# On-chip values for the recurrence, raw x's buffer reused, and decay stored by heads, in a one-core transformer layer

## The chip, the core and the metric

The kernel runs on one core of a Trainium2 chip. A core has five engines with in-order queues: TensorE (PE, matmul; its weight loads are shown as PEld), VectorE (DVE), ScalarE (ACT), GpSimd (POOL) and SyncE (SP), whose queue here issues every DMA. An instruction waits at the head of its queue until the semaphores that it needs are set, and what stands behind it waits too. The metric is the device time of one execution in microseconds (us), the median of several runs.

## The reference

One layer of a hybrid trunk for a sequence of S = 1024 frames of width 1024, in float32. The parts that matter here:

```python
proj = x @ w_in        # q_a k_a v_a f_a | q_b f_b i_b g_b | gate_a gate_b
# attention, 8 heads of 64:
F = cumsum(log_sigmoid(f_a + b_f))                # per head, over frames
p = softmax(causal(q_t.k_s / 8 + F[t] - F[s]))    # y_a = p @ v_a
# recurrence, 4 heads of 128, v = i_b:
f = lb + (1 - lb) * sigmoid(f_b);  k = 1 - f
S_t = diag(f_t) S_{t-1} + k_t v_t^T;  o_t = S_t^T silu(q_t)
y_b = rms_norm(o) * norm_g * sigmoid(g_b)
merged = sigmoid(gate_a) * (y_a @ w_pa) + sigmoid(gate_b) * (y_b @ w_pb)
x = layer_norm(ALPHA * x + merged @ w_o)
x = layer_norm(ALPHA * x + (silu(g) * u) @ w_ff_out)   # u, g = x @ w_ff_in
```

The decay F of attention has one row of 1024 values for each of the 8 heads. Its row for a head is added to every score, so it must stand on all 128 partitions.

## The kernel before

Every matrix is split into a high and a low part (`split`: ACT casts the high part, DVE subtracts it to get the low part), and one product is three matmuls of 128x512 (`mm3`). Large products go by a two by two scheme with seven products (p1 to p7), whose operands are sums and differences of blocks of x and of the weights; DVE makes these. The names of operands: `xh`, `xl` are the parts of x's blocks, `vs1` to `vs4` those of sums of blocks, `T...h`, `T...l` those of weights. `vx`, `vy`, `qk_s`, `qk_pt` and so on are PSUM banks.

The stages, by the trace: projections of the two values (v_a into `va`, i_b into `vbm`) and the forget gates, 0 to 94 us; the q and k projection of head pair 0 (`qk_first`), to about 121; attention, 8 heads, to about 350; the recurrence, 4 heads (`hgrn_project`, `hgrn`), to about 585; gates, branch projections and output projection, to 841; the FFN, to the end. Gate projections (`gate`, PSUM banks `gps`) are also used as filler for TensorE between the products of attention and recurrence.

**What sets the order.** Nothing is issued as written. Each call is recorded by a planner (class `Plan`) with its data dependences, the buffers that it uses and an estimated duration. `schedule` then places the calls one at a time, always the one that can start first by its estimates; ties go by program order. `LAT` is the estimated time until another engine sees a result, `OWN` the same within an engine. Buffers come from slots with a count for each tag ("x" 5, "m" 1, "kb" 4 and so on), and a buffer is placed when a slot of its tag is free. The result is a fixed order for each engine's queue. All recorded calls are issued from one line, L279, so the profile's rows are told apart by the names of tiles.

What the change touches:

- `x2_r` (tag "x", 16 KB on each partition; rows `x_r` in the profile): raw x of the second half of the frames, blocks a21 and a22. The operands for p5, p6, p7 and p3 are made in it, and the splits of a21 for `qk_first` (`xl<-x_r,xh`) are its last use. `box1` (tag "m", four rows of 1024 values) holds the decay rows of attention in two halves, one for even and one for odd heads, and later the values and level buffers of the recurrence. The tag "m" has one slot, and `vbm` has it first.
- `forget_gates`: the forget gates are computed in 8 rows of 512, go through DRAM (`f_d`) to get to 64 rows of 128 (one for each block of 128 frames and head), and are summed along each row by a scan (`nf`). What the blocks ahead add is another sum over the last column: the column goes to DRAM (`b_d`, 64 values), comes back as rows (8 loads of 8x8), is multiplied by a constant table `before` and summed by DVE to `base`. Two more operations on 64x128 (`tensor_scalar` and `scalar_tensor_tensor`) give the decay, which is stored to `nf_d`. All these tiles read `f` in the profile.
- `attention`: for each head one DMA puts that head's decay on all 128 partitions (`box<-nf_d`), from `nf_d` in the order block, head, frame. POOL adds the causal mask to it (`box<-box,causal`), and DVE adds plain or masked decay to the scores: `p<-s,box`, a custom operation that also takes the row's maximum.
- the values of the recurrence: `vbm` is stored to `vb_d`, 8 stores of 256 KB, and each head of the recurrence loads its part into `box1` (512 KB).

Of the kernel before, what the change touches and what calls it, by code (L numbers as in the profile page):

```python
# [7 lines left out]
F32 = mybir.dt.float32  # L8
# [4 lines left out]
ALU = mybir.AluOpType  # L13
# [3 lines left out]
P = 128  # L17
# [35 lines left out]
class Plan:  # L53

    LAT = {"PE": 197.0, "ACT": 131.0, "DVE": 128.0, "POOL": 66.0, "SP": 1950.0}
    OWN = {"PE": 0.0, "ACT": 0.0, "DVE": 127.0, "POOL": 60.0, "SP": 1950.0}
    SETS = {AF.Exp: 0, AF.Ln: 0, AF.Sigmoid: 1, AF.Silu: 2}
# [223 lines left out]
def trunk(ctx: ExitStack, tc, a: dict, out: bass.AP):  # L283
# [175 lines left out]
    load(b22)  # L459
    ax = take("x", [2, 4, NB], "x2_r")  # L460
    a21, a22 = ([ax[:, i, c, :] for c in range(4)] for i in range(2))
    for c in range(4):
# [26 lines left out]

    nf_d = dram.tile([NT, HA, P], F32, name="nf_d")  # L490

    def forget_gates():
# [8 lines left out]
        split(wf[:, :, :HA], wf[:, :, LO:], wfx)  # L501
        f_d = dram.tile([NT, HA, P], F32, name="f_d")
        for hf, ops in enumerate(((A11, A12), (vops["p5"], A22))):
            fo = vx[1 + hf][:LO + HA]
            for c in range(KC):
                h, l = (x[c % 4] for x in ops[c // 4])
                w = wf[:, c + 4 * (hf and c > 3)]
                mm(fo, w, h, start=c == 0, stop=c == KC - 1)
                mm(fo[:HA], w[:, :HA], l, start=False, stop=c == KC - 1, skip_group_check=True)
            fs = half("gt", f"fs{hf}")[:HA]  # L510
            act.copy(fs, fo[LO:])
            dve.tensor_add(fs, fo[:HA], fs)
            sync.dma_start(f_d[4 * hf:4 * hf + 4].rearrange("t h p -> h t p"), fs.rearrange("h (t p) -> h t p", p=P))

# [3 lines left out]
        fz, fa, fe, fu = (f4[:, blk(i)] for i in range(4))  # L518
        sync.dma_start(fa, f_d.rearrange("t h p -> (t h) p"))
        act.activation(fe, fa, AF.Abs, bias=bf, scale=1.0)  # L520
# [34 lines left out]
    forget_gates()  # L555
    product("p5", T1, vy, True)
# [61 lines left out]
    def qk_project(p):  # L618
# [7 lines left out]
        return tiles  # L626

    box1 = take("m", [4, S], "box1")

# [43 lines left out]
    def attention(p, qk):  # L673
        q2, k2, kl = qk
        for i in range(2):
            h = 2 * p + i
            me = slice(i * DH, (i + 1) * DH)

            nfx = box1[:, 2 * (h % 2):2 * (h % 2) + 2, :].rearrange("p a (b c t) -> p (a b) c t", c=2, t=P)
            sync.dma_start(nfx[:, :, 1, :], nf_d[:, h, :].partition_broadcast(P))  # L680
            for hf in range(2):
                b4 = slice(4 * hf, 4 * hf + 4)
                pool.tensor_add(nfx[:, b4, 0, :].rearrange("p (j c) t -> p j c t", c=2),
                                nfx[:, b4, 1, :].rearrange("p (j c) t -> p j c t", c=2),
                                causal[:, None].to_broadcast([P, 2, 2, P]))
            vhl = take("hl", [NT, 2, DH], f"vhl{h}", F32R)
# [3 lines left out]
            for qb in range(NT):  # L690
# [5 lines left out]
                for ci, (c0, w) in enumerate(CHUNKS[qb]):  # L696
# [4 lines left out]
                    for o, m in ((0, w - tail), (w - tail, tail)):  # L701
                        if not m:
                            continue
                        b0, b1 = (c0 + o) // P, (c0 + o + m) // P
                        if o < w - tail:
                            add = nfx[:, b0:b1, 1, :]
                        elif m == P:
                            add = nfx[:, qb:qb + 1, 0, :]
                        else:
                            add = nfx.rearrange("p j c t -> p (j c) t")[:, 2 * qb - 1:2 * qb + 1, :]  # L710
# [804 lines left out]
def _constants():  # L1515
# [12 lines left out]
    t = np.arange(NT * HA)[:, None] // HA  # L1528
    b = np.arange(NT)
    before = np.zeros((NT * HA, NT + 2), np.float32)  # L1530
    before[:, :-2] = (b < t) | (b == t) & (t % 2 == 1)
    before[:, -2:] = np.concatenate([1 - 2 * (t % 2), t % 2], axis=1)
    return {"before": before, "ident": ident, "causal": causal, "once": once,
# [9 lines left out]
def _layout(x, w_in, b_fgate, hgrn_lb_logits, hgrn_norm_g, w_branch_a, w_branch_b, w_out, ln1_g, ln1_b,  # L1543
# [17 lines left out]
    def quarters(m):  # L1561
# [44 lines left out]
```

## Time and profile before

| | us |
|---|---|
| median of 3 runs | 1489.09 |
| lowest, highest run | 1487.78, 1489.48 |
| the profiled execution | 1488.35 |
| its span | 1486.6 |
| TensorE busy | 1455.0 |
| VectorE busy | 1107.8 |
| ScalarE busy | 677.6 |
| GpSimd busy | 99.1 |

The mean granted clock of TensorE over the execution is 0.994 of full speed. The profile is of one execution; its times count from the start of the span. A row of the timeline shows start, duration, engine, operation, the tiles (out<-in) and in brackets the idle time ahead of it with what ended it. A row "x3" stands for three like instructions in a row.

### The profile page before, as it was taken

The numbers are of one execution on the slowest core, as the hardware profiler recorded it, in microseconds if no ns is written. First come the engines' busy times: TensorE is split into PE (matmuls) and PEld (weight loads), VectorE is DVE, ScalarE is ACT, GpSimd is POOL, SyncE is SP. The second block draws the span as 40 slices with busy tenths as digits, with TensorE's granted clock in tenths as the row PEclk, the third lists the DMA queues.
The fourth block names the chain that finished last, engine by engine and source line by source line (L and its number), as shares of the span: only waits on it lengthen the run. The fifth ranks groups of instructions, "written<-read, shape, count | busy, mean of one in ns | idle before, by whom it ended". The sixth has DMA issues, their size and how long they took to land.

```text
span 1486.6 us, 19086 instructions
## 1 busy us (share of the span) xinstructions
PE 1455.0 (98%) x6805; PEld 1191.1 (80%) x6805; DVE 1107.8 (75%) x2090; ACT 677.6 (46%) x1163; POOL 99.1 (7%) x116
## 2 busy tenths in 40 slices
PE   9998999999999999999999899999999999999998
PEld 6766878888887887788888778888888888888887
DVE  7796686776887889744838898666666676798597
ACT  6536576677576575334511343333323323434330
POOL 0003231320001000000001000000000000000000
PEclk9999999999999999999999999999999999999999
DMA  7132232221112234446710203322333334976741
GB/s 261 31 115 79 64 69 48 60 80 40 43 52 77 66 131 157 151 141 212 265 61 1 113 19 117 103 100 102 107 106 106 106 107 170 345 266 219 253 162 58
DMA packets 83472, 177.04 MB, mean 119 GB/s; under 512 B 8816, under 2 KB 22064, under 8 KB 83376
## 3 DMA queue, kind: packets, MB, share of 16 engines
q1 hardware_dynamic: 83376, 175.81, 35.8%
q8 instruction: 54, 0.88, 0.2%
q14 instruction: 42, 0.34, 0.1%
HBM read 136.65 MB, written 39.13 MB: 118 GB/s over the span
## 4 chain that ended last, share of the span: by engine, by line
PE 84%; DVE 9%; DMA 4%; issue 1%; ACT 1%; SPq 1%; POOL 1%; DVEq 0%; ACTq 0%; POOLq 0%
PE p L279 14%; PE fb L279 11%; PE fa L279 8%; PE fc L279 8%; PE bps L279 8%; PE pps L279 6%; PE o L279 6%; PE gs L279 5%; PE gps L279 4%; PE pv L279 2%; PE kps L279 2%; PE s L279 2%; PE pt L279 2%; PE qps L279 2%; DMA b<-in_w_v 1%; PE lp L279 1%
## 5 line engine op out<-in xcount | busy, mean ns | idle before, releaser
L279 PE MATMUL p<-dp 128*128 128x512 f32 (+1 forms) x957 | 210.0, 382 | 0.0
L279 PEld LDWEIGHTS p<-dp 128*128 128x128 f32 x957 | 175.3, 188 | 34.8
L279 PE MATMUL fc<-xs,Tp 128*128 128x512 f32 x528 | 127.0, 389 | 0.0
L279 PE MATMUL fb<-xs,Tp 128*128 128x512 f32 x528 | 126.7, 389 | 0.0
L279 PE MATMUL fa<-x,Tp 128*128 128x512 f32 x480 | 115.7, 389 | 0.3 <-DVE u L279 0.3
L279 PEld LDWEIGHTS fc<-xs,Tp 128*128 128x128 f32 x528 | 99.1, 188 | 20.7 <-ACT xs L279 0.2
L279 PEld LDWEIGHTS fb<-xs,Tp 128*128 128x128 f32 x528 | 99.1, 188 | 20.6
L279 ACT CAST Tp<-t 128x512 fp32r<-128x512 f32 x88 | 54.5, 621 | 115.9 <-PE fc L279 72.6
L279 DVE TENSOR_TENSOR Tp<-t,Tp 128x512 fp32r<-128x512 f32 x88 | 60.7, 691 | 61.7 <-ACT Tp L279 61.2
L279 PEld LDWEIGHTS fa<-x,Tp 128*128 128x128 f32 x480 | 90.0, 188 | 19.3 <-ACT p L279 0.7
L279 ACT CAST dp<-dap 128x1024 fp32r<-128x1024 f32 (+1 forms) x42 | 41.2, 984 | 102.6 <-PE p L279 51.7
L279 PE MATMUL bps<-xl,wb_h 128*128 128x512 f32 x192 | 76.0, 396 | 0.0
L279 PE MATMUL bps<-xh,wb_h 128*128 128x512 f32 x192 | 75.9, 395 | 0.0
L279 PE MATMUL bps<-xh,wb_l 128*128 128x512 f32 x192 | 75.7, 396 | 0.0
L279 POOL TENSOR_TENSOR norm<-norm,mhalf 128x1 f32<-128x1 f32 x16 | 14.6, 914 | 883.8 <-DVE norm L279 883.8
L279 DVE TENSOR_TENSOR tl<-pt,th 128x512 fp32r<-128x512 f32 (+1 forms) x96 | 50.3, 552 | 16.6 <-ACT th L279 16.2
L279 DVE TENSOR_TENSOR dp<-dap,dp 128x1024 fp32r<-128x1024 f32 (+1 forms) x42 | 47.4, 1132 | 15.5 <-ACT dp L279 15.0
L279 POOL TENSOR_SCALAR p<-p,soft 128x384 f32<-128x384 f32 (+4 forms) x64 | 49.1, 772 | 130.2 <-DVE soft L279 113.4
L279 PE MATMUL fb<-x,Tp 128*128 128x512 f32 x240 | 57.7, 389 | 0.0
L279 ACT ACTIVATE p<-p,soft 128x384 f32<-128x384 f32 (+4 forms) x64 | 49.6, 777 | 13.2 <-DVE soft L279 12.9
L279 ACT CAST th<-pt 128x512 fp32r<-128x512 f32 (+1 forms) x96 | 42.9, 479 | 23.2 <-PE pt L279 21.9
L279 ACT CAST Tp<-wg_r 128x512 fp32r<-128x512 f32 x40 | 25.0, 624 | 62.0 <-PE fb L279 32.1
(511 smaller groups left out, 3528.0 us busy)
## 6 DMA issues: line engine op xcount, KB each, us to landing
dbp<-in_w_fo SPq DMA_DIRECT2D x45, 512.0 KB
dap<-a_d SPq DMA_DIRECT2D x35, 512.0 KB
a_d<-ar SPq DMA_DIRECT2D x42, 256.0 KB
wu_r<-in_w_ff SPq DMA_DIRECT2D x20, 512.0 KB
wg_r<-in_w_ff SPq DMA_DIRECT2D x20, 512.0 KB
a_d<-as SPq DMA_DIRECT2D x33, 256.0 KB
wg_r<-in_w_g SPq DMA_DIRECT2D x16, 512.0 KB
sg<-gate_d SPq DMA_DIRECT2D x32, 256.0 KB
```

The source lines that it names most:

```text
L279: getattr(q.engine, method)(*args, **kw)
```

## The change

- `box1` is now raw x's buffer from the start (tag "x", four rows of 1024: rows 0 and 1 hold a21, rows 2 and 3 a22). Even heads of attention use rows 2 and 3 for their decay (plain and masked), odd heads rows 0 and 1. In the recurrence all four rows are level buffers `e`, used in turn.
- `vbm` is read where it is; `vb_d`, its 8 stores and the 4 loads are gone. `vbm` keeps the only slot "m" until the last head's products.
- `f_d` and `nf_d` are stored as 8 rows of 1024. A broadcast reads one row of 4 KB for each partition, where it read 8 pieces of 512 B. The rows of `before`, `bf` and `nf` are sorted by head, then block.
- The round trip by `b_d`, the multiplication and the sum are replaced by one float32 matmul of the table `before` (64x64) with the last column. It goes into a bank of p1 to p7 (`vx[1]`), and is placed, with the two operations that use it, in the loop that ends p3.
- The planner's estimate for the latency of a DMA goes from 1950 to 2500 ns.

```diff
-    LAT = {... "SP": 1950.0}          # OWN the same
+    LAT = {... "SP": 2500.0}
...
-    ax = take("x", [2, 4, NB], "x2_r")
-    a21, a22 = ([ax[:, i, c, :] for c in range(4)] for i in range(2))
+    box1 = take("x", [4, S], "box1")
+    a21, a22 = ([box1[:, 2 * i + c // 2, hs(c % 2)] for c in range(4)] for i in range(2))
...
-    nf_d = dram.tile([NT, HA, P], F32, name="nf_d")
+    nf_d = dram.tile([HA, S], F32, name="nf_d")
...
-        b_d = dram.tile([NT, HA], F32, name="b_d")
-        sync.dma_start(b_d.rearrange("t h -> (t h)").unsqueeze(1), nf[:, P - 1:P])
         dve.tensor_sub(fz, fz, fa)
-        bs = fa[:, :NT]
-        for t in range(NT):
-            sync.dma_start(bs[t * HA:(t + 1) * HA], b_d.rearrange("t h -> h t"))
-        dve.tensor_mul(bs, bs, before[:, :NT])
-        base = fu[:, :1]
-        dve.tensor_reduce(base, bs, axis=mybir.AxisListType.X, op=ALU.add)
-        dve.tensor_scalar(fz, fz, before[:, NT + 1:NT + 2], base, op0=ALU.mult, op1=ALU.add)
-        dve.scalar_tensor_tensor(nf, nf, before[:, NT:NT + 1], fz, op0=ALU.mult, op1=ALU.add)
-        sync.dma_start(nf_d.rearrange("t h p -> (t h) p"), nf)
+        return nf, fz
+
+    def forget_sums(nf, fz):
+        BH = NT * HA
+        base = vx[1][:BH, :1]
+        mm(base, before[:, :BH], nf[:, P - 1:P], start=True, stop=True)
+        dve.tensor_scalar(fz, fz, before[:, BH + 1:BH + 2], base, op0=ALU.mult, op1=ALU.add)
+        dve.scalar_tensor_tensor(nf, nf, before[:, BH:BH + 1], fz, op0=ALU.mult, op1=ALU.add)
+        sync.dma_start(nf_d.rearrange("h (t p) -> (h t) p", p=P), nf)
...
         dve.tensor_add(p1v[t], vx[t], p1v[t])
+        if t == 1:
+            forget_sums(*forget)
         dve.tensor_add(va[:, 4 + t, :], va[:, 4 + t, :], p1v[t])
         dve.tensor_add(vbm[:, 4 + t, :], vbm[:, 4 + t, :], p1v[t])
-    vb_d = dram.tile([NT, P, NB], F32, name="vb_d")
-    for t in range(4, NT):
-        sync.dma_start(vb_d[t], vbm[:, t, :])
     for t in range(4):
         dve.tensor_add(vbm[:, t, :], vy[t], vbm[:, t, :])
-        sync.dma_start(vb_d[t], vbm[:, t, :])
...
-            sync.dma_start(nfx[:, :, 1, :], nf_d[:, h, :].partition_broadcast(P))
+            r = 2 - 2 * (h % 2)
+            nfx = box1[:, r:r + 2, :].rearrange("p a (b t) -> p (a b) t", t=P)
+            sync.dma_start(box1[:, r, :], nf_d[h].partition_broadcast(P))
...
-        vt = box1[:, h % 2, :]
-        sync.dma_start(vt.rearrange("p (t d) -> p t d", d=P), vb_d[:, :, h * P:(h + 1) * P].rearrange("t p d -> p t d"))
...
         def V(w):
-            return vt[:, blk(w)]
+            return vbm[:, w, blk(h)]
...
-            e = box1[:, 2 + li % 2, :]
+            e = box1[:, li % 4, :]
```

The planner turns this into other orders. Three places of the queues, before and after. The first is ACT's queue in `qk_first`, between the casts for q and for k of head pair 0 (`wq` and `wg` are weights of head pair 1 and of the first gate). Before:

```order
90 L279 ACTIVATE q_0_1_201<-qk_s 64x512
91 L279 CAST wq_h_365<-wq_r 128x512
92 L279 CAST k_0_0_202<-qk_u_195 64x512 x2
93 L279 CAST k_0_1_203<-qk_u_195 64x512
94 L279 CAST kl_0_204<-kl_0_204 64x512
```

Now:

```order
91 L279 ACTIVATE q_0_1_198<-qk_s 64x512
92 L279 CAST k_0_0_199<-qk_u_192 64x512 x2
93 L279 CAST k_0_1_200<-qk_u_192 64x512
94 L279 CAST kl_0_201<-kl_0_201 64x512
95 L279 CAST k_0_1_200<-qk_u_192 64x512
...
106 L279 ACTIVATE p_2_224,soft<-p_2_224,soft 128x384
107 L279 CAST wg_0_h_1119<-wg_0_r 128x512
108 L279 CAST wg_0_h_1121<-wg_0_r 128x512
109 L279 CAST wq_h_362<-wq_r 128x512
110 L279 CAST wq_h_364<-wq_r 128x512
111 L279 ACTIVATE p_3_227,soft<-p_3_227,soft 128x512
```

The cast of wq stood ahead of the k casts; both of its halves now stand 17 rows later, behind the casts for the first gate. The second place is DVE's queue around the sums of the forget gates (`f` is every tile of the gates). Before, among the sums for p7 and p3:

```order
93 L279 TENSOR_TENSOR x_r<-x_r,xl_69 128x512
94 L279 TENSOR_TENSOR x_r<-xh_67,x_r 128x512
95 L279 TENSOR_TENSOR f_128<-f_128,before 64x8
96 L279 TENSOR_TENSOR x_r<-xh_67,x_r 128x512
97 L279 TENSOR_REDUCE f_128<-f_128 64x1
98 L279 TENSOR_TENSOR vbm<-vx_73,p1v_106 128x512
99 L279 TENSOR_SCALAR f_128<-f_128,before 64x128
100 L279 TENSOR_TENSOR vs4l_167<-x_r,vs4h_165 128x512
101 L279 SCALAR_TENSOR_TENSOR f_128<-f_128,before 64x128
```

Now, behind the last add of p3 and ahead of the splits of a21:

```order
128 L279 TENSOR_TENSOR vbm<-vy_77,vbm 128x512
129 L279 TENSOR_TENSOR Tqkp2l<-wq_r,Tqkp2h 128x512
130 L279 TENSOR_TENSOR vbm<-vy_78,vbm 128x512
131 L279 TENSOR_SCALAR f_128<-f_128,before,vx_72 64x128
132 L279 SCALAR_TENSOR_TENSOR f_128<-f_128,before 64x128
133 L279 TENSOR_TENSOR xl_68<-box_104,xh_66 128x512 x3
```

The two operations that need the sums stand 32 rows later than before, and the product and the sum on DVE are gone. The third place is SP's queue from the loads for p3 on. Before:

```order
37 L279 DMA x_r<-in_xT 128x512 x2
38 L279 DMA b_d<-f_128 64x1
39 L279 DMA f_128<-b_d 8x8x1 x8
40 L279 DMA nf_d<-f_128 64x128
41 L279 DMA wq_r<-in_w_qk 128x1024
42 L279 DMA wk_r<-in_w_qk 128x1024
43 L279 DMA vb_d<-vbm 128x512 x8
44 L279 DMA box_181<-nf_d 128x8x128 x2
45 L279 DMA wq_r<-in_w_qk 128x1024
46 L279 DMA wg_0_r<-in_w_g 128x1024
```

Now:

```order
37 L279 DMA box_104<-in_xT 128x512 x2
38 L279 DMA wq_r<-in_w_qk 128x1024
39 L279 DMA wk_r<-in_w_qk 128x1024
40 L279 DMA nf_d<-f_128 64x128
41 L279 DMA box_104<-nf_d 128x1024 x2
42 L279 DMA wq_r<-in_w_qk 128x1024
43 L279 DMA wg_0_r<-in_w_g 128x1024
```

The round trip and the stores of `vbm` are gone, and the decay's store now stands behind the loads of the weights of head pair 0, right ahead of the broadcasts.

More of the change, by code (lines that the diff above doesn't have):

```diff
@@ L53 @@
 class Plan:
-    LAT = {"PE": 197.0, "ACT": 131.0, "DVE": 128.0, "POOL": 66.0, "SP": 1950.0}
-    OWN = {"PE": 0.0, "ACT": 0.0, "DVE": 127.0, "POOL": 60.0, "SP": 1950.0}
+    LAT = {"PE": 197.0, "ACT": 131.0, "DVE": 128.0, "POOL": 66.0, "SP": 2500.0}
+    OWN = {"PE": 0.0, "ACT": 0.0, "DVE": 127.0, "POOL": 60.0, "SP": 2500.0}
     SETS = {AF.Exp: 0, AF.Ln: 0, AF.Sigmoid: 1, AF.Silu: 2}
@@ L501, in forget_gates @@
         split(wf[:, :, :HA], wf[:, :, LO:], wfx)
-        f_d = dram.tile([NT, HA, P], F32, name="f_d")
+        f_d = dram.tile([HA, S], F32, name="f_d")
         for hf, ops in enumerate(((A11, A12), (vops["p5"], A22))):
@@ L512, in forget_gates @@
             dve.tensor_add(fs, fo[:HA], fs)
-            sync.dma_start(f_d[4 * hf:4 * hf + 4].rearrange("t h p -> h t p"), fs.rearrange("h (t p) -> h t p", p=P))
+            sync.dma_start(f_d[:, hs(hf)], fs)
         BH = NT * HA
@@ L518, in forget_gates @@
         fz, fa, fe, fu = (f4[:, blk(i)] for i in range(4))
-        sync.dma_start(fa, f_d.rearrange("t h p -> (t h) p"))
+        sync.dma_start(fa, f_d.rearrange("h (t p) -> (h t) p", p=P))
         act.activation(fe, fa, AF.Abs, bias=bf, scale=1.0)
@@ L531, in forget_gates @@
         dve.tensor_tensor_scan(nf, fz, fa, 0.0, op0=ALU.add, op1=ALU.subtract)
-        b_d = dram.tile([NT, HA], F32, name="b_d")
-        sync.dma_start(b_d.rearrange("t h -> (t h)").unsqueeze(1), nf[:, P - 1:P])
         dve.tensor_sub(fz, fz, fa)
-        bs = fa[:, :NT]
-        for t in range(NT):
-            sync.dma_start(bs[t * HA:(t + 1) * HA], b_d.rearrange("t h -> h t"))
-        dve.tensor_mul(bs, bs, before[:, :NT])
-        base = fu[:, :1]
-        dve.tensor_reduce(base, bs, axis=mybir.AxisListType.X, op=ALU.add)
-        dve.tensor_scalar(fz, fz, before[:, NT + 1:NT + 2], base, op0=ALU.mult, op1=ALU.add)
-        dve.scalar_tensor_tensor(nf, nf, before[:, NT:NT + 1], fz, op0=ALU.mult, op1=ALU.add)
-        sync.dma_start(nf_d.rearrange("t h p -> (t h) p"), nf)
+        return nf, fz
[6 more added lines that the diff above has]
+        sync.dma_start(nf_d.rearrange("h (t p) -> (h t) p", p=P), nf)
     bf = const("bf", [NT * HA, 1])
-    before = const("before", [NT * HA, NT + 2])
+    before = const("before", [NT * HA, NT * HA + 2])
     vops["p5"] = A21
@@ L554, in trunk @@
         split(vops["p5"][0][c], vops["p5"][1][c], s1)
-    forget_gates()
+    forget = forget_gates()
     product("p5", T1, vy, True)
@@ L626, in qk_project @@
         return tiles
-    box1 = take("m", [4, S], "box1")
     def qk_first():
@@ L677, in attention @@
             me = slice(i * DH, (i + 1) * DH)
-            nfx = box1[:, 2 * (h % 2):2 * (h % 2) + 2, :].rearrange("p a (b c t) -> p (a b) c t", c=2, t=P)
-            sync.dma_start(nfx[:, :, 1, :], nf_d[:, h, :].partition_broadcast(P))
+            r = 2 - 2 * (h % 2)
+            nfx = box1[:, r:r + 2, :].rearrange("p a (b t) -> p (a b) t", t=P)
+            sync.dma_start(box1[:, r, :], nf_d[h].partition_broadcast(P))
             for hf in range(2):
[L682 to L685, printed above, removed]
+                plain, masked = (nfx[:, b0 + 4 * hf:b0 + 4 * hf + 4].rearrange("p (j c) t -> p j c t", c=2) for b0 in (0, NT))
+                pool.tensor_add(masked, plain, causal[:, None].to_broadcast([P, 2, 2, P]))
             vhl = take("hl", [NT, 2, DH], f"vhl{h}", F32R)
@@ L705, in attention @@
                         if o < w - tail:
-                            add = nfx[:, b0:b1, 1, :]
+                            add = nfx[:, b0:b1]
                         elif m == P:
-                            add = nfx[:, qb:qb + 1, 0, :]
+                            add = nfx[:, NT + qb:NT + qb + 1]
                         else:
-                            add = nfx.rearrange("p j c t -> p (j c) t")[:, 2 * qb - 1:2 * qb + 1, :]
+                            add = nfx[:, qb - 1:NT + qb + 1:NT + 1]
                         res, got = (t.rearrange("p (a t) -> p a t", t=P) for t in (pt[:, c0 + o:c0 + o + m], sc[:, o:o + m]))
@@ L780, in hgrn_project @@
                     dve.tensor_mul(d, o, d)
-        return q, fk, sg, vt
+        return q, fk, sg
     def hgrn(h, qfg, box):
-        q, fk, sg, vt = qfg
+        q, fk, sg = qfg
         k = full("kb", f"hk{h}")
@@ L1527, in _constants @@
             lmask[:, c, nw - 1:2 * nw - 1] = (s[:, None] // (2 * L) == np.arange(nw)) & (s[:, None] // L % 2 == c)
[L1528 to L1532, printed above, removed]
+    bh = np.arange(NT * HA)
+    h, t = bh // NT, bh % NT
+    before = np.zeros((NT * HA, NT * HA + 2), np.float32)
+    before[:, :-2] = (h[:, None] == h) & ((t[:, None] < t) | (t[:, None] == t) & (t % 2 == 1))
+    before[:, -2], before[:, -1] = 1 - 2 * (t % 2), t % 2
     return {"before": before, "ident": ident, "causal": causal, "once": once,
@@ L1582, in _layout @@
         "w_fo": quarters(np.asarray(w_ff_out)[0]),
-        "bf": c(np.tile(np.asarray(b_fgate)[0], NT).reshape(NT * HA, 1)),
+        "bf": c(np.repeat(np.asarray(b_fgate)[0], NT).reshape(NT * HA, 1)),
         "lbl": c(np.asarray(hgrn_lb_logits)[0].reshape(HB, P).T),
```

## The prediction

> **What bounds the kernel now.** First the page: busy times, then the chain of work that ended last.
>
> ```profile
> PE 1455.0 (98%) x6805; PEld 1191.1 (80%) x6805; DVE 1107.8 (75%) x2090; ACT 677.6 (46%) x1163; POOL 99.1 (7%) x116
> PE 84%; DVE 9%; DMA 4%; issue 1%; ACT 1%; SPq 1%; POOL 1%; DVEq 0%; ACTq 0%; POOLq 0%
> ```
>
> TensorE (PE) is busy for 1455.0 of the span's 1486.6 us. No part of the change takes away large matmul work, so at most about 31 us of idle time, and matmuls that ran at a low clock, are there to be had. The second view is the stretches of the program: it shows where that time lies.
>
> ```profile
> 50.00:100.00 50.00, 47.19 (x204) 37.72 (x203) 40.05 (x80) 19.35 (x36) 0.00 (x0) 1.00 0.24 76
> 113.00:119.00 6.00, 0.47 (x3) 0.17 (x1) 1.35 (x2) 1.95 (x4) 2.26 (x2) 0.85 0.40 136
> 119.00:124.00 5.00, 4.83 (x13) 3.75 (x14) 3.70 (x11) 4.85 (x9) 0.00 (x0) 0.50 0.00 0
> 124.00:130.00 6.00, 4.52 (x21) 3.00 (x20) 4.79 (x17) 5.45 (x13) 1.85 (x3) 1.00 0.00 0
> 130.00:350.00 220.00, 219.03 (x1156) 177.62 (x1155) 158.61 (x545) 147.90 (x316) 61.38 (x73) 1.00 0.25 64
> 550.00:600.00 50.00, 48.37 (x254) 39.51 (x253) 48.77 (x95) 26.00 (x59) 3.23 (x2) 1.00 0.47 159
> 900.00:1270.00 370.00, 370.00 (x1634) 306.46 (x1633) 255.78 (x384) 120.33 (x197) 0.00 (x0) 1.00 0.34 113
> ```
>
> Columns: window, length, then busy us of PE, weight load, VectorE (DVE), ScalarE (ACT) and GpSimd (POOL), then granted clock, DMA share, GB/s. Read the first number after the comma. From 130 to 350 us (attention with gate matmuls as filler) and from 900 to 1270 us TensorE is never really idle: time won before 130 us is carried to the end, and work that DVE or DMA lose there is worth nothing. From 113 to 119 us it does almost nothing, and from 119 to 124 us it is busy at half the clock. The third view, PE's waits, names them:
>
> ```profile
> PE s L279 <- ACT k L279: 5.5, 1, 5.5
> PE fa L279 <- ACT Tp_0h L279: 4.1, 1, 4.1
> PE vx L279 <- DVE vbm L279: 1.9, 1, 1.9
> PE qk_s L279 <- DVE vbm L279: 0.8, 1, 0.8
> PE qk_pt L279 <- DVE qk_u L279: 0.7, 1, 0.7
> ```
>
> All but the second lie between 75 and 119 us. The change touches both their roots.
>
> **Term 1: the round trip of the block sums (b_d).** On DVE and SP (rows of the timeline):
>
> ```profile
> 61.49 0.41 DVE L279 TENSOR_TENSOR_SCAN f<-f 64x128 f32<-64x128 f32 x1
> 66.21 0.68 DVE L279 TENSOR_TENSOR x_r<-xh,x_r 128x512 f32<-128x512 f32 x1
> 68.28 2.73 SPq L279 DMA_DIRECT2D f<-b_d  x8
> 75.75 0.16 DVE L279 TENSOR_TENSOR f<-f,before 64x8 f32<-64x8 f32 x1 [8.86 <-DMA f<-b_d]
> 77.11 0.33 DVE L279 TENSOR_SCALAR f<-f,before 64x128 f32<-64x128 f32 x1
> 77.96 0.34 DVE L279 SCALAR_TENSOR_TENSOR f<-f,before 64x128 f32<-64x128 f32 x1
> 109.48 0.69 DVE L279 TENSOR_TENSOR qk_u<-qk_pt,qk_p 128x512 f32<-128x512 f32 x1
> 110.28 0.69 DVE L279 TENSOR_TENSOR qk_u<-qk_s,qk_u 128x512 f32<-128x512 f32 x1
> ```
>
> DVE's in-order queue stands 8.86 us before `f<-f,before`. Behind it are the `vbm<-vx` adds that free PE's banks (1.9 us of PE idle), then everything up to `qk_u`, which DVE works off late (0.8 and 0.7 us more). Changed, a 64x1 matmul gives the sums, and its two users stand some thirty rows later, behind the last `vbm<-vy`. DVE does not wait at 66.9 us any more. It then has about 8 us in hand, more than PE's three waits together, so these go: 1.9 + 0.8 + 0.7 = 3.4 us. From there PE sets the pace, and the second `qk_u` add, done at 110.97 us, is done at about 107.6. What the wait turns into: DVE now waits for the last `vy` product of p3 instead, which it must do in any order.
>
> The added matmul has no row in the trace. From below it costs nothing much (one column); from above, the x128 products `s<-k,q` below took 0.37 us each at half clock, and its inputs (the scan, done near 62 us, and the bank vx[1], read by an add long before) are ready. I take 0.2 us.
>
> **Term 2: the k casts no longer stand behind a weight load.** ACT's and PE's rows:
>
> ```profile
> 108.03 0.60 ACT L279 ACTIVATE q<-qk_s 64x512 fp32r<-64x512 f32 x1
> 117.00 0.62 ACT L279 CAST wq_h<-wq_r 128x512 fp32r<-128x512 f32 x1 [8.37 <-DMA wq_r<-in_w_qk]
> 117.53 1.89 ACT L279 CAST k<-qk_u 64x512 fp32r<-64x512 f32 x3
> 118.84 1.12 PE L279 MATMUL s<-k,q 128*128 128x128 f32 x3 [5.53 <-ACT k L279]
> 128.06 1.13 ACT L279 CAST wg_h<-wg_r 128x512 fp32r<-128x512 f32 x2
> 128.71 0.50 PE L279 MATMUL gps<-xh,wg_h 128*128 128x512 f32 x1 [0.26 <-ACT wg_h L279]
> ```
>
> ACT idles 8.37 us for weights that only the next head pair needs, while the k casts behind it have had their input since 110.97 us. In the changed order both wq_h casts stand after wg_h. The k casts then start when `qk_u` is done: at about 111.1 without term 1 (6.4 us earlier than 117.53), and at about 107.65 with it: 9.9 us earlier.
>
> How much of that reaches the end? From 117.53 to 128.06 us ACT is dense (4.85 of 5 and 5.45 of 6 us busy in the windows): k, kl, softmax, q and wg_h casts in a chain of 10.5 us. The first gate matmul, PE's filler for all that follows, hangs on its last link. Shifted, wg_h starts at about 118.2 and `gps` at 118.8 instead of 128.7: **-9.9 us**. PE has less to do than that chain: its last p7 product ends near 109.9, and the work up to `gps` is 15.4 us (113.3 to 128.7) less idle time (5.53, 0.17 and 1.48 us by the windows) less half of 4.83 us at clock 0.50, so 5.8 us, done by 115.7. So ACT paces the stretch and the clock that returns is hidden behind it.
>
> Here a rule bears on the sum. The Trainium skill, "TensorE: Matmul & The Clock Gate" (What's actually happening), says that an idle window of about 3.4 us halves the clock and a busy one restores it; the trace agrees: 5.53 us idle, then about 5 us at 0.50. By that rule alone the shorter gap would also give back some 2.4 us of PE time; the ACT rows say that it is not on the path. It is a rival below.
>
> One more wq_h cast (starts 0.53 us apart) now stands ahead of the softmax of block 3: 0 to 0.5 us, and ACT has idle time just there; I take 0.2.
>
> **Edits costed at nothing.** The round trip of V (8 stores, 4 loads) lies under attention and recurrence.
>
> ```profile
> 87.95 11.55 SPq L279 DMA_DIRECT2D vb_d<-vbm  x8
> 101.40 1.00 SPq L279 DMA_DIRECT2D box<-nf_d  x2
> 110.05 2.29 POOL L279 TENSOR_TENSOR box<-box,causal 128x512 f32<-128x512 f32 x2 [109.60 <-DMA box<-nf_d]
> 115.73 2.26 POOL L279 TENSOR_TENSOR box<-box,causal 128x512 f32<-128x512 f32 x2 [3.40 <-DMA box<-nf_d]
> 120.78 0.28 DVE L279 CUSTOM_DVE_ANT_0 p<-s,box 128x128 f32<-128x128 f32 x1
> 94.21 0.39 PE L279 MATMUL vy<-Tvp3h,vs4l 128*128 128x512 f32 x1
> 50.86 1.51 DMA f_d<-fs
> ```
>
> SP spends 11.55 us on the stores, with nothing behind them that is late but the broadcasts of the decay. These now have a new chain: last `vy` product at 94.6 - 1.9 = 92.7 us, the last add and the two 64x128 operations (0.69 + 0.33 + 0.34 us), the store (1.5 us as for f_d): issue at about 96. The old broadcast took 8.6 us (101.40 to 110.05) in rows of 512 B. I take the same for rows of 4 KB, since no row shows them; POOL is done at about 107. The first user is `p<-s,box`, now at about 111: 4 us of cover, so zero. If that cover were gone, DVE would stand there with the kl subtractions behind it.
>
> Recurrence and gates: the buffer that held raw x used to be free early; now it serves until level 5 of the last head, so the sums of the gate products come some 50 DVE rows later:
>
> ```profile
> 536.69 0.69 DVE L279 TENSOR_TENSOR xg_r<-xg_r 128x512 f32<-128x512 f32 x1
> 540.53 1.29 DVE L279 TENSOR_TENSOR xg_r<-xg_r 128x512 f32<-128x512 f32 x2 [1.04 <-DMA xg_r<-in_xT]
> ```
>
> That is from 536.7 to 541.7 us some 3.6 us of DVE work and 1 us of wait, moved from a place where it delayed the recurrence into 550 to 600 us, where DVE is full (48.77 of 50) and PE loses 1.6. Bounds: +3.6 (all of it late there) and -2 (what PE's gaps before it can give back). Values in four level buffers instead of two, and no load of V, pull the other way. I take +0.3. The other orders (start of the FFN, the 4.1 us wait) I take as 0, within 1 us either way.
>
> Sum: -9.9 + 0.2 + 0.2 + 0.3 = -9.2 us. The profiled execution took 1488.35 us (median of the runs 1489.09): 1488.35 - 9.2 = **1479.2 us**. Differences under 0.2% (3 us) cannot be told from no change here; the line is at 1486.1.
>
> **Rivals.**
> 1. *Only the weight load goes.* DVE's wait returns in another form (the matmul, or PE's banks, hold it up), and term 1 gives nothing. For it: DVE is dense from 75.8 to 111 us. Against: its 8.9 us in hand are over twice what PE waits. -6.4 + 0.7 = -5.7: 1482.7 us.
> 2. *The clock counts too.* If PE and not ACT paces 110 to 119 us (a filler found sooner), all its loss there returns: 5.53 + 0.17 + 1.48 + 2.4 + 3.4 = 13.0, less 0.7: 1476.1 us. Against it: the ACT chain above. The clock rule cited above speaks for it.
> 3. *The gate sums come too late.* +3.6 us instead of +0.3: 1482.5 us. For it: DVE's 48.77 of 50.
> 4. *Slower: the decay rows become the wait.* All 128 partitions now fetch one row of 4 KB, where they fetched eight of 512 B, and the first use has 4 us of cover. Each us beyond a landing near 108.5 delays DVE, ACT and PE in turn; before gains are gone (`p<-s,box` at 120.78 again) it must land at 118.4 instead of 104.6, 22.4 us after its issue instead of 8.6. At twice the time that both broadcasts now take (101.40 to 115.73, 14.3 us) it would land at 124.7, with POOL 127 and 16 us late: 1488.35 - 9.2 + 16 = 1495 us. Against it: longer rows should not be slower.
>
> **How the numbers follow.** Forecast 0.56, rival 1 0.14, rival 2 0.13, rival 3 0.10, rival 4 0.04, other orders that lose as much as is won 0.03. Forecast's own range 1475 to 1484 (recurrence -2 to +3.6, FFN 1 either way, up to 3 us of clock). The range for 8 in 10 takes in rivals 1 to 3 with their own spread: 1473.5 to 1486. Faster 0.89 (forecast and rivals 1 to 3, less their outer parts), same 0.06, slower 0.05.
>
> **What would show it.** PE's waits lose `vx <- DVE vbm`, `qk_s <- DVE vbm` and nearly all of `s <- ACT k`; DVE has no row that waits for b_d; k casts near 107.6, `p<-s,box` near 111, `gps` near 118.8; the granted clock stays near 1 from 105 to 125. POOL's first masked row is done before DVE asks for it. Wrong it would be if `p<-s,box` waits for POOL or DMA, if PE's idle time between 500 and 620 us grows by more than 3 us, or if a new wait of several us opens in attention.

## The result

| | before | changed |
|---|---|---|
| median of 4 runs, us | 1488.62 | 1479.22 |
| lowest to highest | 1487.78 to 1489.48 | 1477.74 to 1481.75 |
| profiled execution | 1488.35 | 1477.74 |
| its span | 1486.6 | 1475.8 |

The ratio is 0.9939 (95% interval 0.9921 to 0.9956): 9 us faster, by 7 to 12. In a second set of 6 runs it was 1479.49 us, ratio 0.994 (0.9928 to 0.9951). The forecast was 1479.2. The number was right, in part by luck: the stretch before 130 us gave less than forecast, and what comes behind it gave more. First the busy times and the chain of waits of the changed kernel:

```profile
PE 1451.7 (98%) x6807; PEld 1190.5 (81%) x6807; DVE 1109.4 (75%) x2088; ACT 669.3 (45%) x1157; POOL 97.7 (7%) x116
PE 89%; DVE 5%; DMA 2%; ACT 2%; issue 1%; POOL 0%; SPq 0%; DVEq 0%; ACTq 0%; POOLq 0%
```

DVE's and DMA's share of the chain fell (9 and 4% before). PE's waits show what went and what came:

```profile
PE fa L279 <- ACT Tp_0h L279: 4.0, 1, 4.0
PE qk_pt L279 <- DVE qk_u L279: 3.1, 1, 3.1
PE s L279 <- DVE soft L279: 1.2, 1, 1.2
PE gps L279 <- ACT wg_h L279: 1.1, 1, 1.1
```

The waits `s <- ACT k` (5.5 us), `vx <- DVE vbm` (1.9) and `qk_s <- DVE vbm` (0.8) are gone. `qk_pt <- DVE qk_u` has grown from 0.7 to 3.1 us. The same stage by windows (columns as in the prediction):

```profile
106.00:112.00 6.00, 3.57 (x17) 2.95 (x18) 4.49 (x8) 3.43 (x7) 0.00 (x0) 1.00 0.08 31
112.00:118.00 6.00, 4.55 (x22) 3.36 (x21) 4.24 (x17) 5.89 (x13) 0.44 (x2) 1.00 0.00 0
118.00:124.00 6.00, 4.75 (x16) 3.54 (x17) 4.93 (x14) 4.18 (x10) 1.47 (x3) 0.72 0.20 50
124.00:130.00 6.00, 6.00 (x32) 4.74 (x31) 4.06 (x13) 2.93 (x7) 1.01 (x2) 1.00 0.38 129
550.00:600.00 50.00, 48.34 (x231) 38.66 (x230) 46.34 (x82) 27.66 (x59) 3.90 (x2) 1.00 0.46 156
```

PE's one idle stretch of 5.5 us has become several shorter ones (3.1, 1.2 and 1.1 us), ACT is dense from 112 to 118 us, and the clock still drops, later and for less long: by the records of the granted clock it was 0.50 from 117.22 to 124.05 us before, and is so from 120.21 to 123.62 us now. The rows on the path, from the timeline of ACT, PE and DVE:

```profile
109.12 1.91 ACT L279 CAST k<-qk_u 64x512 fp32r<-64x512 f32 x3 [2.37 <-DVE qk_u L279]
120.38 1.14 ACT L279 CAST wq_h<-wq_r 128x512 fp32r<-128x512 f32 x2
120.00 0.64 PE L279 MATMUL gps<-xh,wg_h 128*128 128x512 f32 x1 [1.12 <-ACT wg_h L279]
112.38 0.28 DVE L279 CUSTOM_DVE_ANT_0 p<-s,box 128x128 f32<-128x128 f32 x1
91.13 0.27 PE L279 MATMUL vx<-f,before 64*64 64x1 f32 x2
```

The k casts start 8.4 us sooner (117.53 before), the first gate matmul 8.7 us sooner (128.71). The 64x1 matmul costs 0.27 us. Then GpSimd's and DVE's rows just ahead of the k casts, the new thing in this profile:

```profile
98.55 6.31 POOL L279 TENSOR_TENSOR box<-box,causal 128x512 f32<-128x512 f32 x4 [98.11 <-DVE qk_p L279]
98.43 0.68 DVE L279 TENSOR_TENSOR Tqkp6l<-wqk_t,Tqkp6h 128x512 fp32r<-128x512 f32 x1
99.03 1.65 DVE L279 TENSOR_TENSOR wq_r<-wq_r,wqk_t 128x512 f32<-128x512 f32 x1
100.61 1.65 DVE L279 TENSOR_TENSOR vhl<-va,vhl 128x512 fp32r<-128x512 f32 x1
102.19 1.65 DVE L279 TENSOR_TENSOR Tqkp4l<-wq_r,Tqkp4h 128x512 fp32r<-128x512 f32 x1
103.76 1.65 DVE L279 TENSOR_TENSOR Tqkp7l<-wq_r,Tqkp7h 128x512 fp32r<-128x512 f32 x1
105.44 0.68 DVE L279 SCALAR_TENSOR_TENSOR q<-qk_s,q 64x512 fp32r<-64x512 f32 x1
```

Four like DVE operations take 1.65 us in place of 0.69, just while GpSimd adds the causal mask for heads 0 and 1. Before, the same adds ran at 110.05 and 115.73 us; the first pair met the two `qk_u` adds, which read PSUM and took 0.69 (the earlier one in its last 0.1 us only), and most of the second met an idle DVE.

### The profile page after: what moved, and what is told of

Its sections match the earlier page's. It is cut to its first block, busy times and chain, and to the rows that moved or that the text cites. A ratio compares the mean times of both kernels' runs of the same rounds, so it can differ in the third digit from the quotient of the medians.

```text
span 1475.8 us, 19031 instructions
## 1 busy us (share of the span) xinstructions
PE 1451.7 (98%) x6807; PEld 1190.5 (81%) x6807; DVE 1109.4 (75%) x2088; ACT 669.3 (45%) x1157; POOL 97.7 (7%) x116
## 4 chain that ended last, share of the span: by engine, by line
PE 89%; DVE 5%; DMA 2%; ACT 2%; issue 1%; POOL 0%; SPq 0%; DVEq 0%; ACTq 0%; POOLq 0%
PE p L279 14%; PE fb L279 11%; PE fc L279 8%; PE bps L279 8%; PE fa L279 8%; PE pps L279 6%; PE o L279 6%; PE gps L279 5%; PE gs L279 5%; PE vx L279 3%; PE s L279 2%; PE pv L279 2%; PE kps L279 2%; PE pt L279 2%; PE qps L279 2%; PE vy L279 1%
## 5 line engine op out<-in xcount | busy, mean ns | idle before, releaser
L279 PE MATMUL gps<-xh,wg_h 128*128 128x512 f32 x128 | 52.2, 408 | 1.1 <-ACT wg_h L279 1.1
```

The source lines that it names most:

```text
L279: getattr(q.engine, method)(*args, **kw)
```

## The experiments

Twelve kernels ran in three sets (r1, e1, e4, e5; then e2, e3, e7, e9; then e12, e13, e16, e17), each set on one chip together with the kernel before: 1488.76, 1488.46 and 1488.11 us. A gain below is the difference of the medians within a set; the ratios have their intervals.

| run | what it is | median us | gain us | ratio to before (95%) |
|---|---|---|---|---|
| r1_after | the change again | 1479.49 | 9.3 | 0.9940 (0.9928 to 0.9951) |
| e1_lat_only | before, latency 2500 | 1477.59 | 11.2 | 0.9931 (0.9919 to 0.9943) |
| e13_matmul_lat1950 | before, matmul for b_d | 1482.82 | 5.3 | 0.9963 (0.9950 to 0.9976) |
| e3_matmul_only | before, latency 2500 and matmul | 1474.47 | 14.0 | 0.9903 (0.9889 to 0.9916) |
| e2_lat1950 | the change, latency 1950 | 1482.58 | 5.9 | 0.9960 (0.9947 to 0.9972) |
| e4_bd_back | the change, b_d back | 1478.13 | 10.6 | 0.9932 (0.9921 to 0.9944) |
| e5_pool_late | the change, mask adds later | 1477.18 | 11.6 | 0.9922 (0.9910 to 0.9934) |
| e16_pool_later | the same, head 1's later still | 1476.99 | 11.1 | 0.9923 (0.9911 to 0.9936) |
| e7_rows512 | the change, rows of 512 B | 1479.36 | 9.1 | 0.9944 (0.9930 to 0.9957) |
| e9_warm | e5, other adds, 14 matmuls | 1479.49 | 9.0 | 0.9937 (0.9924 to 0.9949) |
| e17_later_warm | e16, 14 matmuls, order kept | 1477.35 | 10.8 | 0.9926 (0.9912 to 0.9940) |
| e12_matmul_warm | e3, 14 matmuls, order kept | 1473.28 | 14.8 | 0.9898 (0.9884 to 0.9911) |

**The change again (r1_after).** No edit.

> The changed kernel again, beside the variants on the same chip, as their reference. Expected: 1479 us (1477 to 1482), 9 us under the kernel before; k casts at 109.1 us, first gate product near 120.0.

Measured 1479.49 us (1478.18 to 1482.12). Its profiled execution, 1482.12 us, is the longest of these, and shows a part of what spreads them. A window and a PE row of it:

```profile
105.00:112.00 7.00, 3.88 (x12) 2.83 (x11) 5.49 (x8) 3.39 (x6) 0.48 (x1) 0.72 0.34 116
109.06 0.77 PE L279 MATMUL qk_pt<-vs3h,Tqkp7h 128*128 128x512 f32 x1 [3.12 <-DVE qk_u L279]
```

After the same 3.1 us wait for `qk_u`, here the clock dropped at once: the 12 matmuls of p7 start 0.43 us apart (109.62, 110.05, ...), where the first profile has 0.23, and the first scores come at 114.32 us instead of 111.26, though the k casts were started at 109.74. This execution was 0.62 us behind the first already ahead of the wait, so the drop cost 2.4 us there. The first gate matmul comes at 122.44 instead of 120.00. The clock was 0.50 from 108.02 to 114.85 us and once more from 121.67 to 128.50; in the first profile only from 120.21 to 123.62. A drop within p7 alone does not make an execution long: the profile of e7_rows512 has one (0.50 from 109.00 to 112.41 us), no other before 800 us, and it ended as early as the first profile (1477.71 us).

Why the same wait costs clock in one execution and not in another can be read from the traces. In each of the 14 profiles the low stretches start whole multiples of 3.41 us apart and last 3.41 or 6.83 us (the last one runs to the end of the program), so the clock is set in steps of 3.41 us. Of the steps at full clock ahead of the last matmul, all 26 in which PE was busy for 1.45 us or less were followed by a low one, and none in which it was busy for more than 2.05 us; between these it went both ways. In r1_after most of the wait falls into one step (104.61 to 108.02 us, PE busy 1.33 us); in the first profile it is split over two (103.14 to 106.56, busy 2.16 us, and to 109.97, busy 1.54 us). Where the steps lie differs from execution to execution.

**Mask adds later (e5_pool_late).** GpSimd gets a two-element add ahead of each head's mask adds, whose input comes late:

```diff
+                late[0] = f(T[1])[:, 3, :2]      # in qk_first, low part of p7's weights
+        late[1] = p1[:, :2]                      # in qk_first, last sum for q
+            if h in late:                        # in attention, ahead of the mask adds
+                pool.tensor_add(box1[:, r + 1, :].rearrange("p (a b) -> p a b", a=2)[:, :, 0], late[h], late[h])
```

> The changed kernel, with GpSimd's adds of the causal mask for heads 0 and 1 made to start later: a two-element add on GpSimd that reads the low part of p7's weights (head 0) or the last sum for q (head 1) writes into the masked row first. Order on all other engines as in the changed kernel. Theory (GpSimd's adds slow DVE's additions of two SBUF tensors): the four DVE rows that took 1.65 us from 99.0 to 105.4 take 0.69 again, qk_u is done near 106.0 instead of 109.1, PE's 3.1 us wait for qk_u is gone, and 2 to 3 us are won: 1476 to 1477 us. Rival (the four rows were slowed by something else, the broadcasts' writes or the weight loads): they stay at 1.65 us, and the time stays at 1479.

GpSimd's and DVE's rows of that run:

```profile
102.45 2.74 POOL L279 TENSOR_TENSOR box<-box,causal 128x512 f32<-128x512 f32 x2
99.19 0.68 DVE L279 TENSOR_TENSOR wq_r<-wq_r,wqk_t 128x512 f32<-128x512 f32 x1
99.80 0.68 DVE L279 TENSOR_TENSOR vhl<-va,vhl 128x512 fp32r<-128x512 f32 x1
100.57 0.69 DVE L279 TENSOR_TENSOR Tqkp4l<-wq_r,Tqkp4h 128x512 fp32r<-128x512 f32 x1
101.41 0.69 DVE L279 TENSOR_TENSOR Tqkp7l<-wq_r,Tqkp7h 128x512 fp32r<-128x512 f32 x1
102.85 1.32 DVE L279 TENSOR_TENSOR vhl<-va,vhl 128x512 fp32r<-128x512 f32 x1
105.72 0.69 DVE L279 TENSOR_TENSOR qk_u<-qk_s,qk_u 128x512 f32<-128x512 f32 x1
```

All four are back at 0.69. The slow one is now the one `vhl` (two inputs from SBUF) that meets the moved adds; the q and `qk_u` operations beside it, with one input from PSUM, stay at 0.69. The k casts start at 106.45, PE's wait for `qk_u` is 0.3 us, and the median is 2.3 us lower. The intervals of the two ratios overlap, but all five runs (1474.95 to 1477.99) lie under all six of r1_after (1478.18 to 1482.12). PE's order is not quite that of the changed kernel: some 30 rows between 119 and 132 us, gate matmuls and transposes, change places; the k casts come before that. The theory holds, the rival is out. The Trainium skill, "SBUF — State Buffer" (SBUF: two separate sides), has it as a rule: DVE and GpSimd share a pair of ports, and a DVE operation with two SBUF inputs excludes a GpSimd operation that reads SBUF and the other way round, for a whole instruction. The trace agrees: the operations alternate, one of each in 1.58 us (6.31 us for four).

**Latency alone (e1_lat_only).** The kernel before, with one line of the change:

```diff
-    LAT = {... "SP": 1950.0}          # OWN the same
+    LAT = {... "SP": 2500.0}
```

> The kernel before with nothing but the planner's SP latency 2500 instead of 1950. ACT's k casts no longer stand behind the cast of wq; the b_d round trip, the stores of V and the 512 B broadcasts stay. Theory (term 2 alone): k casts start at about 111.1 instead of 117.5, first gate product at about 122.3, 1482 to 1483 us (6 us won). Rival (the wait moves to the decay rows or another load): less than 3 us won, with a new wait on DVE or PE before 125 us.

Measured: a gain of 11.2 us, as much as the whole change brings. Neither theory nor rival had that. Two rows:

```profile
110.35 1.91 ACT L279 CAST k<-qk_u 64x512 fp32r<-64x512 f32 x3 [2.37 <-DVE qk_u L279]
121.67 0.50 PE L279 MATMUL gps<-xh,wg_h 128*128 128x512 f32 x1 [1.12 <-ACT wg_h L279]
```

The k casts are 7.2 us sooner and the first gate matmul 7.0, near what was expected (6.4). The rest is won after that. The path from the first gate matmul to the first branch projection (`pps`) in four profiles, before, this run, latency and matmul, and the change:

```profile
128.71:660.46 531.75, 524.93 (x2693) 430.83 (x2694) 403.45 (x1017) 330.48 (x626) 78.48 (x90) 1.00 0.27 82
121.67:651.41 529.74, 526.01 (x2694) 432.63 (x2695) 403.25 (x1018) 335.63 (x631) 77.91 (x90) 1.00 0.27 81
119.61:648.54 528.93, 525.21 (x2693) 432.95 (x2694) 402.71 (x1018) 335.76 (x631) 78.39 (x90) 1.00 0.27 81
120.00:650.96 530.96, 526.64 (x2694) 432.24 (x2695) 402.31 (x1018) 322.81 (x621) 75.65 (x90) 1.00 0.24 77
```

The second number is the length, the third PE's busy time. PE's idle time in this path is 6.8 us before, 3.7 us with the latency alone, 3.7 with the matmul too, 4.3 in the change. The latency figure also sets the order of recurrence and gates, and the order that it gives leaves 3 us less idle time there; 2.0 us of that reach `pps`.

**b_d back (e4_bd_back).** The changed kernel with the round trip; the rows stay sorted by head, so each of the 8 loads now reads a row of 32 B:

```diff
+        b_d = dram.tile([HA, NT], F32, name="b_d")
+        sync.dma_start(b_d.rearrange("h t -> (h t)").unsqueeze(1), nf[:, P - 1:P])
...
+            sync.dma_start(bs[h * NT:(h + 1) * NT], b_d[h].partition_broadcast(NT))
```

> The changed kernel with the b_d round trip in place of the 64x1 matmul, at its old place; all else as changed, SP latency 2500. Theory (term 1): DVE's wait of about 9 us at 67 us returns, with PE's waits for vbm (1.9 and 0.8 us); the decay is stored near 78 us, so the broadcasts and GpSimd's adds come about 10 us sooner, where they slow DVE as well. k casts at 111 to 114, 1482 to 1484 us. Rival (the matmul's gain was eaten by GpSimd's adds altogether): k casts near 109, 1479 to 1480 us.

Measured 1478.13 us: no slower than the change. DVE waited 4.6 us for b_d (8.9 in the kernel before, whose loads were 8 values of 4 B each), and PE's waits for `vbm` did not come back. The decay was ready sooner, so the mask adds of head 0 ran at 84.7 us, where they hit one DVE operation (1.65 us) that had time, and only those of head 1 hit the stretch before `qk_u`. The rival's place came out (k casts at 108.64 us) and nearly its number, but this run can't settle term 1: the loads and the place of the adds changed with it.

**Latency back (e2_lat1950).** The changed kernel with the figure at 1950.

> The changed kernel with the planner's SP latency back at 1950. The cast of wq stands ahead of the k casts again; matmul for the sums, 4 KB broadcasts and values on chip stay. Theory now (the move of the wq cast, made by the latency figure alone, is the change's whole gain by the end): k casts wait for wq again, until some 10 us after its issue at 102, so near 112 to 113 instead of 109; 3 to 4 us of the 9.3 are lost: 1482 to 1483 us. Rival (the rest of the change has its own gain and wq comes early enough to hold nothing): 1479 us.

Measured 1482.58 us, as expected, and for another reason.

```profile
107.95 0.62 ACT L279 CAST wq_h<-wq_r 128x512 fp32r<-128x512 f32 x1
121.85:656.26 534.41, 528.72 (x2693) 434.47 (x2694) 402.58 (x1017) 322.03 (x620) 76.08 (x90) 0.99 0.24 77
```

The cast of wq does stand ahead of the k casts again, but it starts at 107.95 us and holds nothing: wq was issued at 103.3 us and is there by then, where before it was issued at 106.5 and took 10.5 us. The k casts start at 110.30; from the first p3 matmul (`vy`) on that is 29.0 us, as in the change. What is lost lies in the later stages: 534.4 us from the first gate matmul (121.85) to `pps` (656.26), against 531.0. Some 1.1 us of this are clock, low for 6.83 us behind the gate matmul as in r1_after, where this path takes 532.1 us. The other 2.3 us come with the order: PE is idle for 5.7 us in the path, against 4.3, and the clock falls once more, at 581.98 us.

**Matmul on top of the latency (e3_matmul_only).** The run with the latency alone, with `forget_sums` of the change (rows sorted by block, as before):

```diff
+        base = vx[1][:BH, :1]
+        mm(base, before[:, :BH], nf[:, P - 1:P], start=True, stop=True)
```

> The kernel before with latency 2500 (as in the run with the latency alone) and the 64x1 matmul in place of the b_d round trip, at the place that the change gives it; the stores of V and the broadcasts in 512 B rows stay. Theory (term 1): PE's waits for vbm and qk_u before the k casts go, k casts near 106.5 instead of 110.4. The 512 B broadcasts start only at 97 to 100 us and take 8.6 us, so the masked rows are done near 110 to 112, when DVE wants them: 1 to 3 us of the 3.9 reach the end, 1475 to 1477 us. Rival (term 1 gives nothing even where GpSimd doesn't disturb DVE): k casts at 110, 1477.6 us as with the latency alone.

This is the clean pair for term 1: all queues but for some 25 rows are the same. Measured 1474.47 us, just under the range of the theory and 3 us under the latency alone (ratios 0.9903 and 0.9931: 4 us). Three rows:

```profile
108.37 1.91 ACT L279 CAST k<-qk_u 64x512 fp32r<-64x512 f32 x3 [2.79 <-DVE qk_u L279]
105.52 2.30 POOL L279 TENSOR_TENSOR box<-box,causal 128x512 f32<-128x512 f32 x2 [105.08 <-DMA box<-nf_d]
112.76 1.59 DVE L279 TENSOR_TENSOR kl<-qk_p,k 64x512 fp32r<-64x512 f32 x1 [0.30 <-ACT k L279]
```

The k casts are only 2.0 us sooner than with the latency alone, since in this profile the clock was 0.50 from 30.93 to 34.34 us, ahead of all this. In e12 below, with the same order up to there and no such drop, they start at 106.60, as expected, and the first gate matmul comes at 117.84, 3.8 us sooner than with the latency alone. Here the broadcasts come later (issued at 97.2 behind the stores of V), and the adds of head 0 meet q and `qk_u`, which are not slowed. The later pair slows one `kl`. With the whole memory part of the change still missing, this kernel is 5 us faster than the change.

**Matmul alone (e13_matmul_lat1950).** The same with the latency at 1950.

> The kernel before with the 64x1 matmul alone, SP latency at 1950: the fourth of the two by two of latency and matmul. The cast of wq stands ahead of the k casts, and DVE doesn't wait for b_d. Theory (the k casts wait for wq's landing, some 10.5 us after an issue at about 104, whatever comes ahead): k casts near 115, gain 2 to 3 us, 1485 to 1486 us. Rival (the matmul gives its 4 us in any case): 1484 us or less.

Measured a gain of 5.3 us: by the number the rival, not the theory's 2 to 3 us. The theory's place was right, though, since the wq cast holds the k casts:

```profile
112.49 0.62 ACT L279 CAST wq_h<-wq_r 128x512 fp32r<-128x512 f32 x1 [6.69 <-DMA wq_r<-in_w_qk]
```

They start at 113.02 us, 4.5 sooner than before, since wq itself is issued sooner (104.7) and lands in 7.7 us. So latency and matmul overlap: 11.2 and 5.3 us alone, 14.0 together (the 2.5 us of overlap are not clear of the intervals). Both shorten the same wait of the k casts, and so does (as the run with the latency back shows) the memory part of the change, by which wq lands in 4 us.

**Rows of 512 B (e7_rows512).** The decay is stored with a gap, so that a broadcast reads 512 B at a time:

```diff
-    nf_d = dram.tile([HA, S], F32, name="nf_d")
+    nf_d = dram.tile([HA, NT, 2 * P], F32, name="nf_d")
-            sync.dma_start(box1[:, r, :], nf_d[h].partition_broadcast(P))
+            sync.dma_start(nfx[:, :NT], nf_d[h, :, :P].partition_broadcast(P))
```

> The changed kernel with the decay stored in pieces of 512 B (each followed by 512 B of gap), so that a broadcast reads eight of 512 B for each partition instead of one of 4 KB. Theory (long rows make the broadcast quick, and so GpSimd's adds early): the first masked row starts near 103 to 104 us instead of 98.6, the adds fall on other DVE rows (q and qk_u read PSUM and stay at 0.69, vhl does not), k casts near 107, and the time is the same or 1 us less: 1478 to 1479. Rival (row length does not matter): GpSimd's adds start at 98.6 as before.

```profile
98.92 6.35 POOL L279 TENSOR_TENSOR box<-box,causal 128x512 f32<-128x512 f32 x4 [98.48 <-DVE qk_p L279]
```

The theory falls: with rows of 512 B the adds start at 98.92 instead of 98.55, about 4 us after the issue at 94.8, and the time is the same (1479.36). What made the old broadcasts take 8 us is something else, the stores of V in flight just before or the distance of the pieces in DRAM (4 KB then, 1 KB here); these were not told apart.

**Keeping PE busy (e9_warm, e12_matmul_warm, e17_later_warm; e16_pool_later as base).** The added lines; in e12 and e17 the planner counts these matmuls at no time:

```diff
+        warm, kl = bank("h", "warm"), tiles[2][1]
+        for _ in range(14):
+            mm(warm, kl[:, :P], kl[:, hs(1)], start=True, stop=True)
```

> The run with GpSimd's adds made late, with two more edits: the adds for head 1 start only after the last write of head pair 0's q, and 14 matmuls 128x512 whose result nobody reads stand between the first scores and the first softmax transposes, waiting for the last kl cast, so that PE is busy from about 114 to 117 us. Theory (PE's idle time there lets the clock drop to half for some 5 us from 118 on, while PE is the bound): granted clock stays near 1 from 112 to 124 and 2 us are won beside the run with late adds: 1475 us. Rival (the clock drops anyway, or the added matmuls hold up the transposes): 1477 us or more.

The clock stayed at 1.00 from 112 to 130 us, and the run was 5 us ahead of e5 by the first recurrence projection (319.1 against 324.3). But the added time in the plan had changed the order of everything later: PE then waited 4.5 us for `ob` and lost 4.8 us from 550 to 600. 1479.49 us: nothing won.

> The run with latency 2500 and the matmul alone, with 14 matmuls added whose result nobody reads (128x512, waiting for the last kl cast), which the planner counts at no time, so that every queue keeps the order of that run. Theory (the half clock near 120 us costs PE time that is on the path from then on): granted clock near 1 from 112 to 124 instead of 0.72 at the end, 1.5 to 2 us won: 1472.5 to 1473 us against 1474.5. Rival (those 2 us are hidden by a wait later, in attention): no change, 1474.5.

With the order of e3 kept, the windows of that run:

```profile
112.00:118.00 6.00, 5.59 (x29) 4.64 (x28) 4.70 (x17) 5.89 (x15) 1.44 (x3) 1.00 0.00 0
118.00:124.00 6.00, 5.87 (x30) 4.58 (x30) 5.19 (x17) 3.63 (x8) 1.33 (x3) 1.00 0.43 143
```

Clock 1.00, 0.72 in e3, and 1473.28 us against 1474.47: 1.2 us, in the direction and near the size of the theory. The intervals overlap, and by the gains within the sets it is 0.8 us, so the size is not shown. This is the fastest kernel of the study, 14.8 us under the kernel before and 5.5 to 6 under the change.

> The run with GpSimd's adds made late, with head 1's adds later still: they wait for the last write of head pair 0's q, so GpSimd's first softmax scalings no longer stand behind them. Only GpSimd's queue differs. Theory (in that run PE's waits of 1.9 us for GpSimd's p deepened the clock's drop): PE's waits for p are gone, clock from 118 to 124 at 0.7 or more instead of 0.56, 1476 us against 1477.2. Rival: no change.

1476.99 us and a clock of 0.72 from 118 to 124; beside e5 no difference that can be told.

> The run before this one (the whole change, GpSimd's adds at other times) with the 14 added matmuls that the planner counts at no time; order otherwise the same. Theory of the clock: 1474 us, 2 us under the run without them, and within 1.5 us of the run with latency, matmul and added matmuls. Rival (the values on chip and the reused buffer cost time of their own in recurrence and gates): 1476 us or more.

1477.35 us, with the clock at 1.00: no gain over e16. The rival's number comes out: the whole change, with mask adds out of DVE's way and the clock kept, is still 4 us behind e12. The path from the first gate matmul to `pps` of e16, to set beside the four above:

```profile
117.68:649.20 531.52, 527.07 (x2694) 432.38 (x2694) 403.99 (x1018) 323.03 (x621) 79.22 (x92) 1.00 0.24 77
```

It is 2.6 us longer than in e3, of which 0.7 are idle time of PE; the rest lies between matmuls that count as busy, spread over attention, recurrence and gates with no wait of its own. That the reused buffer causes it (by the order that the planner makes of it) is not shown.

## Why the number was right, and where the steps were not

**The total** was -9.2 us forecast, -9.4 measured. The parts, by the profiles (two single executions, so with about 1 us of doubt each): up to the first gate matmul -8.7 (forecast -9.5), from there to `pps` -0.8 (+0.3), from `pps` to the end -1.3 (0). That the total fits to 0.2 us is luck. The last part is mostly clock: behind PE's wait for `fa` it was 0.50 for 6.83 us before (from 844.26 us) and for 3.41 us here (from 837.00); r1_after, with 6.83 us there, takes 825.7 us from `pps` to the end, 0.4 less than before.

**Term 1 (b_d): mechanism right, size right where it stands alone, and then eaten.** Forecast 3.4 us of PE waits. On top of the latency figure the matmul alone brought 3 to 4 us (e3 against e1). In the change PE did gain more than that ahead of `qk_u` (the last p3 matmul came at 104.92, 4.3 us sooner than 109.23), and then lost 3.1 us to the new wait for `qk_u`. The sentence that failed is "from there PE sets the pace": DVE set it again, for four operations at 1.65 us. So the k casts came at 109.12 us where 107.65 was forecast, and `p<-s,box` and `gps` 1.2 to 1.4 us late with them.

**Term 2 (the wq cast): right place, two more roots than seen.** The k casts no longer wait for wq, ACT's chain of 10.9 us from there to `gps` paces the stretch as argued (109.12 to 120.00), and the 64x1 matmul and the second wq cast cost as little as said. But the prediction put the gain to the order alone. e2 shows that with the memory part of the change the old order would do as well, since wq then lands in 4 us. And it priced the latency figure at that one place, while alone it brought 11.2 us; of these the profiles show 7.0 up to `gps`, 2.0 from there to `pps` and 0.3 behind it (the profiled execution of e1 is 1.4 us above its median).

**"Edits costed at nothing": wrong.** The sum took the decay's broadcasts as hidden because the first user had 4 us of cover. The cover was there: the adds were done at 104.9 us, the first use came at 112.38. The broadcasts landed 4.0 us after their issue, where the sum took 8.6, so the adds came early. What was not asked is what GpSimd's adds do to the engine beside them when they run 11 us sooner. That cost 2.3 us (e5), of the 5 us that separate the change from latency and matmul alone; the other 2.5 to 3 are in the later stages and stay open.

**Recurrence and gates: +0.3 forecast, -0.8 measured, the sum of two things.** The bound by the late gate sums (+3.6) didn't come: PE's idle time from 550 to 600 us is 1.66 us, as before (1.63). The order that comes with the latency figure alone shortened the path from `gps` to `pps` by 2.0 us; in the change 0.8 of that are left.

**Rivals.** Only the weight load goes (1482.7): out, the `vbm` waits are gone. The clock counts too (1476.1): half right. ACT paced the stretch in the first profile, as argued, but the sign that the clock stays near 1 from 105 to 125 us did not come, and in r1_after the clock fell within the p7 products and PE paced them, which cost 2.4 us there. The spread of the change (ten runs, 1477.7 to 1482.1) is wider than that of e3 (four runs, 1473.5 to 1474.8), where that wait is missing, but e1 without it spreads as far (1476.9 to 1480.6): the wait is not the only cause. By the rule of the Trainium skill that the prediction cited, "TensorE: Matmul & The Clock Gate" (What's actually happening), an idle window of 3.4 us is wanted and the windows run free of the kernel. The traces agree with the free windows (steps of 3.41 us, placed otherwise in each execution), and differ on the idle one: the clock fell after steps in which PE was busy for 1.3 us (r1_after) and more. Late gate sums and late decay rows: out.

## What to carry to other kernels

A buffer that comes free sooner lets work start sooner, and that work can land beside something critical: price not only when a moved instruction ends but which engine it shares a port with while it runs. A number in a planner is a change of its own: test it alone first, since here one line brought as much as the whole change, and what came with it hid a loss of 5 us. And when two edits shorten the same wait, their gains don't add; a two by two of runs tells it at the cost of three kernels.

## What the runs showed of the hardware

- A DVE operation 128x512 with both inputs in SBUF takes 1.65 us instead of 0.69 beside GpSimd's 128x512 additions, which in turn take 1.58 instead of 1.15 us each; a DVE operation with one input in PSUM keeps its 0.69 us.
- PE's granted clock fell to 0.50 for 3.41 or 6.83 us at a time, in steps of 3.41 us that lie otherwise in each execution. It fell after each step at full clock in which PE was busy for at most 1.45 us, and after none with more than 2.05 us, so a wait of 3.1 us halved it in one execution and not in another; 14 matmuls that nobody reads kept it at full speed through a stretch of idle time.
- Broadcasts of one 4 KB row to 128 partitions landed in about 4 us, and as fast in pieces of 512 B 1 KB apart; with the stores of V ahead of them and pieces 4 KB apart they took about 8.
